# Value products of two attentions emitted per pair of heads, alternating between the two 64-row halves of the output

## The chip, the core and the metric

The kernel runs on one NeuronCore of one Trainium2 chip. The metric is the device time of one execution in microseconds. Before the change it is 2310.92 us, the median of 3 runs (2307.32 to 2318.86). Engines are called PE (TensorE; PEld is its weight load), DVE (VectorE), ACT (ScalarE), POOL (GpSimd) and SP (SyncE, which issues most transfers).

## What is computed

Two transformer blocks run one after the other over 256 tokens of width 1024, with 256 context tokens. The first block has two layers (an even one with an mLSTM mixer, an odd one with windowed attention), each between two gated feed-forward networks. The second block joins a latent attention with a state-space scan and ends in a convolutional feed-forward network. The change touches the two attentions:

- Odd layer: 16 query heads of 64 dimensions share 4 key and value heads. Each block of 128 queries sees 256 context keys and up to 256 keys of its own stream (a window of 128 each way). The softmax has one more term per head, a learned sink.
- Latent attention: 16 heads with scores over 64 + 32 dimensions, values of 64 dimensions, 512 keys, and no sink.

In both, one head's output for 128 queries is

```
p = softmax(scores)        # 128 queries x 512 keys
out = p @ v                # 512 keys x 64 value dimensions
```

and the outputs of all heads go through an output projection.

## The kernel before, in words

Nearly all matrix products of the program are made of three products of float32r halves (`mac3`, lines 580 to 584: high by high, high by low, low by high). The transposes and the value products work on plain float32.

**A unit of attention** is one head with 128 queries. Each attention has 32 units, made by the local function `unit` (line 1558 in `odd`, line 2195 in `mla`) in the order pair of heads, query block `qb`, head `s` of the pair, so that the units `s = 0` and `s = 1` of a pair follow each other. `attention` (line 1416) runs them as a software pipeline whose stages are written in a string:

```
AO = "s0 e1 n1 t3 v4 f0"
```

In iteration i it emits `st0` of unit i (the scores, lines 1567 to 1570 or 582 to 584, then the row maximum on DVE, L1427), `st1` of unit i-1 (the exponential on ACT, L1436, and with a sink L1439 and L1440), `st2` of unit i-1 (reciprocal and scaling on DVE, L1444 and L1445), `st3` of unit i-3 (four transposes on PE, L1451, and their copy out of PSUM on ACT, L1453, which makes the tile `PT`), `st4` of unit i-4 (the value products) and then other work that was put beside the attention (`fill`: in `odd` the modulation of the second block's context, in `mla` the projections of queries, keys and values and their weights).

**Value products** (L1578 and L2213): four matmuls of a unit, one for each block of 128 keys. The stationary operand is a slice of 64 columns of `V`, the moving operand a slice of 128 columns of `PT`, both 128 partitions of float32. The result has 64 rows, in the lower half (rows 0 to 63) of the PSUM tile `po` for `s = 0` and in the upper half (rows 64 to 127) for `s = 1`:

```
for b in range(4):
    nc.tensor.matmul(po[64 * s:64 * s + 64, ...], lhsT=V[b][:, kv * 64:kv * 64 + 64],
                     rhs=PT[:, b * P:(b + 1) * P], start=b == 0, stop=b == 3, tile_position=(0, 64 * s), ...)
```

The profile shows each such float32 matmul as two instructions, so a unit's value products are eight. After 8 units `po` is full and is split into float32r halves for the output projection (`split`, lines 604 and 605).

A third place writes into halves of PSUM in the same way: `y` in `ssd` (lines 2335 to 2350) computes outputs of the state-space scan from the same kinds and sizes of operands (L2349). Its innermost loop is the one over `s`, so its matmuls go to the lower and the upper half in turn.

**Order and buffers.** The engines' instructions are placed when the program is built: instructions are taken in the order of emission as far as a model of that moment holds them ready, so an instruction whose input is late is passed by later ones. Blocks of [128, 512] (`b2`, 42 buffers, line 334) hold `PT`, the probabilities, keys, queries and values; `mm` (5 banks) and `aux` (2 banks) are the PSUM tiles of scores and transposes. `po` takes one bank of `bg` and one of `mm` in turn (line 395).

Of the kernel before, what the change touches and what calls it, by code (L numbers as in the profile page):

```python
# [56 lines left out]
P = 128  # L57
# [11 lines left out]
# ---------------------------------------------------------------- host layout  # L69
# [44 lines left out]
def _pack_tok(w):  # L114
    """Pieces of 4 blocks of rows by 512 columns, the column halves one after the other."""
    kb = w.shape[0] // P
    parts = []
    for c in range(2):
        for k0 in range(0, kb, 4):
            t = w.reshape(kb, P, D)[k0:k0 + 4, :, c * 512:(c + 1) * 512].transpose(1, 0, 2)  # L120
            parts.append(np.ascontiguousarray(t).reshape(-1))
    return np.concatenate(parts)
# [174 lines left out]
# ---------------------------------------------------------------- the program  # L297
# [5 lines left out]
class Beat:  # L303
    """Emission order of work that waits on long chains: after(k, f) emits f once k more blocks of products are out."""
# [23 lines left out]
class Prog:  # L328
# [18 lines left out]
    @contextmanager  # L347
    def in_order(self):
        """Each compute engine issues what this block emits in the order of its emission."""
        ins = self.nc.cur_bb.bb.instructions  # L350
        n = len(ins)
        yield
        self.tails = {}
        for i in list(ins[n:]):
            if i.engine != mybir.EngineType.SP:
                if i.engine in self.tails:
                    self.issue_behind(i, self.tails[i.engine])
                self.tails[i.engine] = i

    @contextmanager  # L360
    def behind_now(self):
        """What this block emits is issued behind what has been emitted."""
        ins = self.nc.cur_bb.bb.instructions
        n = len(ins)
        last = {i.engine: i for i in ins[-200:]}
        yield
        for i in list(ins[n:]):
            if i.engine in last:
                self.issue_behind(i, last[i.engine])

    @contextmanager
    def behind(self):
        """What this block emits is issued behind the last block in order."""
        ins = self.nc.cur_bb.bb.instructions
        n = len(ins)
        yield
        for i in list(ins[n:]):
            if i.engine in self.tails:
                self.issue_behind(i, self.tails[i.engine])

    # ---- tiles
# [13 lines left out]
    def po(self):  # L395
        """Accumulators of attention outputs, alternating between two pools."""
        self.npo = getattr(self, "npo", 0) + 1
        if self.npo % 2:
            return self.gp.tile([P, 512], F32, tag="bg", name=self.name("bg"))
        return self.mm()  # L400

    def scope(self, name):
        """A pool for one phase; self.sp is the pool that phase allocates from."""
        self.sp_es = ExitStack()
        self.sp = self.sp_es.enter_context(self.tc.tile_pool(name=name, bufs=1))
# [43 lines left out]
    # ---- modulation vectors  # L449
# [5 lines left out]
    def mods(self, ci, w, bias, M, i0, cnt, post):  # L455
        """Steps that compute modulation vectors i0 .. i0+cnt-1 of M, one weight slab each."""
# [41 lines left out]
    def mods_acc(self, ci, w, bias, M, i0, cnt, post, nctx):  # L498
        """Like mods, with the products summed over weight slabs on VectorE and only the last sum, over
        partitions, on the tensor engine. nctx: how many of the vectors the context stream uses."""  # L500
# [42 lines left out]
    def tick(self, n=1.0):  # L543
        """Emit background steps worth n."""
# [11 lines left out]
    # ---- weights: hi + lo, each exact in float32r  # L556
    def wload(self, src, nk, width, pool=()):
        """pool: the pieces whose lo part GpSimd computes."""
# [27 lines left out]
    def pair3(self, ps, W, X, first, last):  # L586
        """Both halves of one block of rows, the products that need the lo part of X behind the others."""
# [19 lines left out]
    # ---- rms statistics of one half (256 tokens), features on partitions  # L607
# [23 lines left out]
    def rstd2(self):  # L631
        """r1 = rms(h)^-1 and r12 = r1 * rms(h * fin * r1)^-1, as columns r12, r12, r1, r1.

        With a = mean h^2 + eps and b = mean (h fin)^2: r12 = (b + eps a)^-1/2."""
# [15 lines left out]
    def chunk(self, half, t, c):  # L650
        """Features 512 c.. of the tokens 128 t.., tokens on partitions, in the place of 2 blocks of h."""
        return self.h[:, 4 * c + 2 * t:4 * c + 2 * t + 2, HS[half]]

    def finish_first(self):
        """h_x = rms(h_x) * fin, the result of the first block, with tokens on partitions from here on."""
# [12 lines left out]
    def gain(self, i, cs=range(2)):  # L668
        """Gate times gain of the second block, along the free axis."""
# [24 lines left out]
    def tok_gemm(self, acts, src, evac, tail=None):  # L694
        """Products with tokens on partitions: evac(t, c, ps) of tokens 128 t.. and columns 512 c.. .

        tail(products) takes over before the last pieces, where products(t) emits those of t."""
# [39 lines left out]
    def modulate(self, acc, srcs, sc, sh, X, n=D):  # L737
        """X[k] = split(src[k] * sc[k] * rstd + sh[k]) over one half."""
# [46 lines left out]
    def start(self, X):  # L785
        """Loads, the first norm and its modulation (a quarter of the features at a time), and the products of
        the first two hidden blocks over each quarter as it becomes ready. Returns their accumulators."""
# [135 lines left out]
    # ---- swiglu over both streams  # L923
# [74 lines left out]
    # ---- one-stream feed forward: act(j, psum[:, 2, 256]) -> (hi, lo)  # L998
# [40 lines left out]
    # ---- even mixer  # L1039
    def even(self, X, M, half_done):  # L1040
# [18 lines left out]
        # q, k (convolved, feature-major); gates first  # L1059
# [12 lines left out]
        k = []  # L1072
# [25 lines left out]
        # output gate and spatial gating unit, in pieces that run between the mlstm steps  # L1098
# [84 lines left out]
        def out_s(m):  # L1183
            """The part of the output that the gating unit feeds."""
# [11 lines left out]
        def out_m(half, m):  # L1196
            """The part of the output that the mlstm feeds, over one half."""
# [26 lines left out]
    def mlstm_gates(self, G):  # L1224
        """Row-wise gate arithmetic. Rows 0-3 forward heads, rows 32-35 backward heads."""
# [60 lines left out]
    def mlstm(self, q, k, v, gates, hs):  # L1286
# [22 lines left out]
        def prep(n):  # L1309
            """What a step needs apart from the running state."""  # L1310
# [73 lines left out]
    # ---- odd mixer (x stream queries; keys of both streams)  # L1384
# [6 lines left out]
    def rope_mul(self, x, rows, tab, n):  # L1391
        """x [rows, n, 256] f32 in SBUF -> its two rotated terms."""
# [23 lines left out]
    def attention(self, units, pre, order):  # L1416
        """Software-pipelined attention. A unit is 128 queries of one head against 512 keys:
        (scores() -> PSUM, (sink, -sink) columns or None, values(PT)); pre[n] runs before unit n's scores."""
# [54 lines left out]
    def odd(self, X, M, before, half_done):  # L1473
# [84 lines left out]
        def unit(a_, g, qb, s):  # L1558
# [14 lines left out]
            def values(PT):  # L1573
                if (g % 2, qb, s) == (0, 0, 0):
                    hold["po"] = self.po()
                po = hold["po"]
                for b in range(4):
                    nc.tensor.matmul(po[64 * s:64 * s + 64, (g % 2) * 256 + qb * P:(g % 2) * 256 + qb * P + P],  # L1578
                                     lhsT=V[b][:, kv * 64:kv * 64 + 64], rhs=PT[:, b * P:(b + 1) * P],
                                     start=b == 0, stop=b == 3, tile_position=(0, 64 * s), skip_group_check=True)  # L1580
                if (g % 2, qb, s) == (1, 1, 1):
# [25 lines left out]
    # ---- second block: conv5 + silu of one xbc feature block  # L1607
# [13 lines left out]
    def ssd_gates(self, ps):  # L1621
        """Rows 0-15 forward dt, rows 32-47 backward dt, [128, 256 tokens]."""
# [13 lines left out]
        # per-token columns: -acum, dt, dt * exp(acum_end - acum); per-chunk exp(acum_end) on all partitions  # L1636
# [33 lines left out]
    def xs_tok(self, xs, c, g):  # L1670
        """Token-major heads of group g, chunk c, in PSUM [128 tokens, 8, 64]."""
# [31 lines left out]
    def in_half(self, srcname, i, b, X, W):  # L1703
        """One 128-feature block of an input projection; W keeps the weights of the slab."""
# [28 lines left out]
    def block2_setup(self):  # L1733
        nc = self.nc
        # silu(t) = u (1 + tanh u) with u = t / 2: the convolution yields u
# [22 lines left out]
    def norm_later(self, bt, k, acc, srcs, sc, X, n):  # L1758
        """X = split(src * sc * rstd), its statistics k beats from now, the rest a beat after that."""
# [18 lines left out]
    def ctx_stats(self):  # L1778
        """Steps that leave 1 / rms of the second block's context in rc."""
# [11 lines left out]
    def ctx_path(self):  # L1791
        """Everything of the second block's context that its x stream reads, in pieces."""
# [329 lines left out]
    def mla(self, CQ, tab):  # L2122
# [72 lines left out]
        def unit(pair, qb, s):  # L2195
# [10 lines left out]
            def values(PT):  # L2206
                if (pair % 2, qb, s) == (0, 0, 0):
                    hold["po"] = self.po()
                po = hold["po"]
                hd = (2 * pair + s) % 8  # L2210
                col = (pair % 2) * 256 + qb * P
                for tb in range(4):
                    nc.tensor.matmul(po[64 * s:64 * s + 64, col:col + P], lhsT=V[pair // 4, tb][:, hd * 64:hd * 64 + 64],  # L2213
                                     rhs=PT[:, tb * P:(tb + 1) * P], start=tb == 0, stop=tb == 3,
                                     tile_position=(0, 64 * s), skip_group_check=True)
                if (pair % 2, qb, s) == (1, 1, 1):
# [54 lines left out]
    def ssd(self, xs, B, Cm, ac, TA, DD, DE):  # L2271
        """State-space scan of the x stream, in pieces: cb, xd_a(g, c), xd_b(g, c), unit(n), mix(n), y(n)."""
# [62 lines left out]
        def y(n):  # L2335
            """Outputs of the units n and n + 1."""
# [22 lines left out]
    # ---- the whole computation  # L2359
    def run(self):  # L2360
# [104 lines left out]
        # the final norm of the first block folds into the norm of the second  # L2465
# [36 lines left out]
```

## Time and profile before

| | |
|---|---|
| runs shown | 2307.32, 2310.92, 2318.86 us; median 2310.92 |
| profiled execution, span from first to last instruction | 2305.9 us; its own device time is not listed beside it |
| median over the span | 5.0 us |
| mean granted TensorE clock | 0.991 of 2.4 GHz |
| PE, DVE, ACT busy | 97%, 68%, 42% of the span |
| odd attention, first to last value product | 1459.3 to 1532.0 us |
| latent attention, first to last value product | 1988.6 to 2079.7 us |

The span and the stretches are of one profiled execution. A share of busy time is an average over stages with different limits, so the two attentions are read by themselves, in stretches and in the order of PE's instructions. In a timeline a row with xN stands for N instructions in a row on one line; the duration of such a row reaches to the end of the last one, and since matmuls overlap in the pipeline, the time that a row takes from the stream is the distance from its start to the next row's start.

### The profile page before, as it was taken

Reading aid. Unit: us, or ns where it says so; the run is one execution under the profiler, and the core shown is the slowest. Engines: PE = TensorE matmul, PEld = TensorE weight load, DVE = VectorE, ACT = ScalarE, POOL = GpSimd, SP = SyncE. Lnnn points to the kernel's source line nnn. Section 1 sums busy time; section 2 is a strip of 40 time slices with the busy share of each in tenths; the row PEclk is TensorE's granted clock in tenths of the full one; section 3 lists DMA queues with packets and bytes.
Section 4 is the critical chain, followed back from the end, with each engine's and each line's share of the span. In section 5 each row is a group of like instructions: output and inputs, shape, how many; then the busy total and the mean of one; then the engine's idle time right before and its main releaser. Section 6 shows DMA issues by size and latency. Waiting matters only on the chain.

```text
span 2305.9 us, 33864 instructions
## 1 busy us (share of the span) xinstructions
PE 2247.0 (97%) x13706; PEld 1956.2 (85%) x13706; DVE 1564.9 (68%) x2447; ACT 975.2 (42%) x1651; POOL 166.7 (7%) x185
## 2 busy tenths in 40 slices
PE   7999999999899999999999999999999899999998
PEld 6888888888898888898878889789999788888997
DVE  5887774734897666468748647757556898666664
ACT  4222223544542222243222335656445566665553
POOL 0000000001300000000000002101000553000000
PEclk8999999999999999999999999999999999999999
DMA  7665552221145455325657623114554323213553
GB/s 266 218 232 182 185 204 83 92 101 74 56 160 187 155 192 183 146 92 201 242 173 285 231 92 115 57 56 169 184 183 160 133 88 122 85 60 126 184 175 120
DMA packets 58076, 348.54 MB, mean 151 GB/s; under 512 B 6464, under 2 KB 10048, under 8 KB 22848
## 3 DMA queue, kind: packets, MB, share of 16 engines
q1 hardware_dynamic: 56544, 344.22, 42.1%
q8 instruction: 108, 1.77, 0.3%
q0 software_dynamic: 512, 1.05, 0.2%
q10 hardware_dynamic: 864, 1.11, 0.2%
q14 instruction: 48, 0.39, 0.0%
HBM read 343.73 MB, written 1.05 MB: 150 GB/s over the span
## 4 chain that ended last, share of the span: by engine, by line
PE 76%; issue 13%; DVE 5%; POOL 3%; ACT 1%; DMA 1%; SPq 0%; POOLq 0%; DVEq 0%; ACTq 0%
PE mm L582 21%; PE mm L584 20%; PE mm L583 20%; PE mm L591 6%; PE ax L1451 1%; DVE wl L575 1%; POOL b L1727 1%; PE bg L531 1%; PE bg L1578 1%; PE bg L2213 1%; PE mm L1578 1%; PE mm L2213 1%; DMA b<-mod 1%; POOL b L1728 1%; DVE acc L616 0%
## 5 line engine op out<-in xcount | busy, mean ns | idle before, releaser
L582 PE MATMUL mm<-b,wh 128*128 128x512 f32 (+1 forms) x2764 | 958.5, 348 | 3.6 <-DVE c L1617 1.9
L584 PE MATMUL mm<-b,wl 128*128 128x512 f32 (+1 forms) x2764 | 947.7, 344 | 3.6 <-DVE wl L575 3.5
L583 PE MATMUL mm<-b,wh 128*128 128x512 f32 (+1 forms) x2764 | 949.5, 344 | 0.0
L575 DVE TENSOR_TENSOR wl<-wr,wh 128x1024 fp32r<-128x1024 f32 (+2 forms) x474 | 553.7, 1173 | 392.0 <-ACT wh L574 385.5
L574 ACT CAST wh<-wr 128x1024 fp32r<-128x1024 f32 (+2 forms) x474 | 473.7, 1006 | 575.8 <-PE mm L583 389.8
L582 PEld LDWEIGHTS mm<-b,wh 128*128 128x128 f32 x2764 | 527.0, 191 | 78.3 <-issue 8.5
L584 PEld LDWEIGHTS mm<-b,wl 128*128 128x128 f32 x2764 | 526.1, 191 | 65.7 <-DVE wl L575 5.0
L583 PEld LDWEIGHTS mm<-b,wh 128*128 128x128 f32 x2764 | 527.3, 191 | 61.0 <-issue 1.9
L522 DVE SCALAR_TENSOR_TENSOR ma<-mr,cs,ma 128x1024 f32<-128x1024 f32 x252 | 311.5, 1278 | 32.9 <-DMA mr<-ada 28.8
L591 PE MATMUL mm<-b,wh 128*128 128x256 f32 x1408 | 254.5, 283 | 0.0
L591 PEld LDWEIGHTS mm<-b,wh 128*128 128x128 f32 x1408 | 220.3, 192 | 0.2 <-ACT b L604 0.2
L591 PE MATMUL mm<-b,wl 128*128 128x256 f32 x704 | 184.4, 283 | 0.0
L591 PEld LDWEIGHTS mm<-b,wl 128*128 128x128 f32 x704 | 135.5, 192 | 0.0
L927 ACT ACTIVATE s<-mm 128x512 f32<-128x512 f32 x66 | 39.5, 599 | 222.2 <-PE mm L584 222.1
L582 PE MATMUL mm<-wh,b 128*128 128x512 f32 (+1 forms) x264 | 100.1, 380 | 1.9 <-ACT b L604 1.9
L583 PE MATMUL mm<-wl,b 128*128 128x512 f32 (+1 forms) x264 | 99.5, 377 | 0.0
L584 PE MATMUL mm<-wh,b 128*128 128x512 f32 (+1 forms) x264 | 99.3, 377 | 0.0
L629 POOL TENSOR_TENSOR rr<-rv,nhalf 128x2 f32<-128x2 f32 x15 | 15.6, 1043 | 991.6 <-DVE rv L628 991.6
L604 ACT CAST b<-s 128x512 fp32r<-128x512 f32 x70 | 43.2, 617 | 73.4 <-DVE s L928 64.9
L928 DVE TENSOR_TENSOR s<-s,mm 128x512 f32<-128x512 f32 x66 | 45.2, 684 | 40.3 <-PE mm L584 40.3
L1427 DVE TENSOR_REDUCE mx<-mm 128x1 f32<-128x512 f32 x64 | 43.8, 687 | 31.9 <-PE mm L1570 17.5
L983 DVE SCALAR_TENSOR_TENSOR h<-mm,M,h 128x256 f32<-128x256 f32 x144 | 59.6, 476 | 7.5 <-PE mm L584 7.5
(357 smaller groups left out, 2072.8 us busy)
## 6 DMA issues: line engine op xcount, KB each, us to landing
wr<-win SPq DMA_DIRECT2D x88, 1024.0 KB, 4.8
mr<-ada SPq DMA_DIRECT2D x56, 1024.0 KB, 4.9
wr<-wout SPq DMA_DIRECT2D x40, 768.0 KB, 4.4
mr<-mod SPq DMA_DIRECT2D x26, 1024.0 KB, 5.0
wr<-b_up SPq DMA_DIRECT2D x22, 1024.0 KB, 4.9
wr<-wout SPq DMA_DIRECT2D x14, 1024.0 KB, 4.8
wr<-b_xbc SPq DMA_DIRECT2D x11, 1024.0 KB, 4.9
wr<-b_down SPq DMA_DIRECT2D x10, 1024.0 KB, 4.9
```

Of the source, the lines that this page charges most:

```text
L522: nc.vector.scalar_tensor_tensor(hold["a"][s][:, c], raw[:, c], v, hold["a"][s][:, c], op0=ALU.mult, op1=ALU.add)
L574: nc.scalar.copy(hi, r)
L575: (nc.gpsimd if k0 // kk in pool else nc.vector).tensor_sub(lo, r, hi.bitcast(F32))
L582: nc.tensor.matmul(ps, lhsT=ah, rhs=bh, start=first, stop=False)
L583: nc.tensor.matmul(ps, lhsT=ah, rhs=bl, start=False, stop=False)
L584: nc.tensor.matmul(ps, lhsT=al, rhs=bh, start=False, stop=last)
L591: nc.tensor.matmul(ps[:, HS[q]], lhsT=l[:, P * q:P * q + P], rhs=r, start=first and q == 0 and l is wh and r is xh, stop=last and q == 1 a ...
L928: nc.vector.tensor_mul(s, s, pu)
L983: nc.vector.scalar_tensor_tensor(h[:, m, c], ps[:, c], M[:, ig, m, half:half + 1], h[:, m, c], op0=ALU.mult, op1=ALU.add)
L1427: nc.vector.tensor_reduce(mx, S[u], axis=AX.X, op=ALU.max, negate=True)
L1578: nc.tensor.matmul(po[64 * s:64 * s + 64, (g % 2) * 256 + qb * P:(g % 2) * 256 + qb * P + P], lhsT=V[b][:, kv * 64:kv * 64 + 64], rhs=PT[: ...
L2213: nc.tensor.matmul(po[64 * s:64 * s + 64, col:col + P], lhsT=V[pair // 4, tb][:, hd * 64:hd * 64 + 64], rhs=PT[:, tb * P:(tb + 1) * P], st ...
```

## The change

`values` of a unit `s = 0` now issues nothing and only keeps its `PT`. `values` of the unit `s = 1` issues the products of both: for each block of 128 keys first the one into the lower half, then the one into the upper half. The number of matmuls, their operands and sizes are the same. `po` is taken and split at the same places in the order of units. Other lines of the diff drop comments and docstrings; they change no instruction.

```diff
@@ odd, unit
             def values(PT):
-                if (g % 2, qb, s) == (0, 0, 0):
+                if s == 0:
+                    hold["PT"] = PT
+                    return
+                if (g % 2, qb) == (0, 0):
                     hold["po"] = self.po()
                 po = hold["po"]
+                col = (g % 2) * 256 + qb * P
                 for b in range(4):
-                    nc.tensor.matmul(po[64 * s:64 * s + 64, (g % 2) * 256 + qb * P:(g % 2) * 256 + qb * P + P],
-                                     lhsT=V[b][:, kv * 64:kv * 64 + 64], rhs=PT[:, b * P:(b + 1) * P],
-                                     start=b == 0, stop=b == 3, tile_position=(0, 64 * s), skip_group_check=True)
-                if (g % 2, qb, s) == (1, 1, 1):
+                    for z, t in enumerate((hold["PT"], PT)):
+                        v = (2 * a_ + z) * 64
+                        nc.tensor.matmul(po[64 * z:64 * z + 64, col:col + P], lhsT=V[b][:, v:v + 64],
+                                         rhs=t[:, b * P:(b + 1) * P], start=b == 0, stop=b == 3,
+                                         tile_position=(0, 64 * z), skip_group_check=True)
+                if (g % 2, qb) == (1, 1):
...
@@ mla, unit
             def values(PT):
-                if (pair % 2, qb, s) == (0, 0, 0):
+                if s == 0:
+                    hold["PT"] = PT
+                    return
+                if (pair % 2, qb) == (0, 0):
                     hold["po"] = self.po()
                 po = hold["po"]
-                hd = (2 * pair + s) % 8
                 col = (pair % 2) * 256 + qb * P
                 for tb in range(4):
-                    nc.tensor.matmul(po[64 * s:64 * s + 64, col:col + P], lhsT=V[pair // 4, tb][:, hd * 64:hd * 64 + 64],
-                                     rhs=PT[:, tb * P:(tb + 1) * P], start=tb == 0, stop=tb == 3,
-                                     tile_position=(0, 64 * s), skip_group_check=True)
-                if (pair % 2, qb, s) == (1, 1, 1):
+                    for z, t in enumerate((hold["PT"], PT)):
+                        hd = (2 * pair + z) % 8
+                        nc.tensor.matmul(po[64 * z:64 * z + 64, col:col + P],
+                                         lhsT=V[pair // 4, tb][:, hd * 64:hd * 64 + 64], rhs=t[:, tb * P:(tb + 1) * P],
+                                         start=tb == 0, stop=tb == 3, tile_position=(0, 64 * z), skip_group_check=True)
+                if (pair % 2, qb) == (1, 1):
```

## Rows read from the trace of the kernel before

**Rows 1.** The page: span, busy time and instructions by engine, clock in 40 slices.

```profile
span 2305.9 us, 33864 instructions
...
PE 2247.0 (97%) x13706; PEld 1956.2 (85%) x13706; DVE 1564.9 (68%) x2447; ACT 975.2 (42%) x1651; POOL 166.7 (7%) x185
...
PEclk8999999999999999999999999999999999999999
```

**Rows 2.** The page, the chain that ended last: its shares by engine.

```profile
PE 76%; issue 13%; DVE 5%; POOL 3%; ACT 1%; DMA 1%; SPq 0%; POOLq 0%; DVEq 0%; ACTq 0%
```

**Rows 3.** Stretches: us, busy PE, PEld, DVE, ACT, POOL, clock, DMA share, GB/s.

```profile
1459.27:1531.96 72.68, 72.68 (x486) 54.84 (x486) 46.93 (x164) 48.56 (x129) 0.00 (x0) 1.00 0.04 16
1988.59:2079.66 91.07, 91.07 (x583) 73.63 (x583) 60.03 (x127) 60.71 (x130) 6.39 (x12) 1.00 0.21 67
```

**Rows 4.** PE's timeline in the odd attention: start us, duration us, instruction, count.

```profile
1506.21 0.50 PE L1567 MATMUL mm<-b,b 128*128 128x512 f32 x1
1506.56 0.23 PE L1568 MATMUL mm<-cstb 128*128 128x128 bf16 x1
...
1507.14 0.60 PE L1451 MATMUL ax<-cst,b 128*128 128x128 f32 x4
1507.67 1.09 PE L1578 MATMUL bg<-b,b 128*64 128x128 f32 x8
1508.69 0.50 PE L1567 MATMUL mm<-b,b 128*128 128x512 f32 x1
```

**Rows 5.** PE's timeline, the same in the latent attention.

```profile
2060.59 0.60 PE L1451 MATMUL ax<-cst,b 128*128 128x128 f32 x4
2061.12 1.09 PE L2213 MATMUL bg<-b,b 128*64 128x128 f32 x8
...
2062.94 0.60 PE L1451 MATMUL ax<-cst,b 128*128 128x128 f32 x4
```

**Rows 6.** Waits in the odd attention: who waited for whom, us in total, times, longest.

```profile
DVE mx L1427 <- PE mm L1570: 17.5, 21, 2.6
ACT b L1453 <- PE ax L1451: 17.0, 22, 1.3
...
PEld bg L1578 <- ACT b L1453: 0.7, 2, 0.4
```

**Rows 7.** PE's timeline in the odd attention, where a unit's products came apart.

```profile
1493.33 0.65 PE L1578 MATMUL mm<-b,b 128*64 128x128 f32 x4
1493.92 0.66 PE L1451 MATMUL ax<-cst,b 128*128 128x128 f32 x4
```

**Rows 8.** PE's timeline in the state-space scan, the alternating products of L2349.

```profile
1882.85 1.97 PE L2349 MATMUL mm<-b,b 128*64 128x128 f32 x32
1884.74 0.49 PE L728 MATMUL ax<-cst,rr 128*128 128x128 f32 x2
```

**Rows 9.** PE's timeline at the odd attention's end, two units in one run.

```profile
1530.31 1.71 PE L1578 MATMUL mm<-b,b 128*64 128x128 f32 x16
1531.96 0.38 PE L583 MATMUL mm<-b,wh 128*128 128x256 f32 x1
```

**Rows 10.** PE's timeline in the odd attention, transposes with scores right behind them.

```profile
1480.08 0.60 PE L1451 MATMUL ax<-cst,b 128*128 128x128 f32 x4
1480.44 0.47 PE L1567 MATMUL mm<-b,b 128*128 128x512 f32 x1
1480.76 0.23 PE L1568 MATMUL mm<-cstb 128*128 128x128 bf16 x1
```

**Rows 11.** Busy us by stretch, columns as in rows 3: quiet, dense, scan.

```profile
1506.21:1523.52 17.31, 17.31 (x113) 12.95 (x113) 10.78 (x37) 10.82 (x30) 0.00 (x0) 1.00 0.01 1
...
1468.59:1490.30 21.72, 21.72 (x144) 16.38 (x143) 17.98 (x60) 17.36 (x46) 0.00 (x0) 1.00 0.11 39
1990.00:2060.00 70.00, 70.00 (x437) 56.80 (x436) 48.67 (x101) 48.67 (x105) 5.46 (x10) 1.00 0.26 84
...
1880.00:1950.00 70.00, 70.00 (x678) 65.45 (x677) 61.45 (x102) 44.75 (x108) 26.28 (x22) 1.00 0.32 109
```

## The prediction

> **What bounds the kernel.** I read the page first: PE is busy 97% of a span of 2305.9 us, DVE 68%, ACT 42%, and the clock stands at its upper level (2.4 GHz) nearly throughout [rows 1]. The chain that ended last is PE for 76% and issue for 13% [rows 2]. Whole-program shares say nothing of one stage, so I took busy time by stretch, from the first to the last value product of each attention: PE has no idle time in either (72.68 of 72.68 us, 91.07 of 91.07), while ACT and DVE are busy 65 to 67% of each, at clock 1.00 [rows 3]. PE's timeline shows why. In the odd attention a unit is scores, mask, four transposes and eight value products back to back, 2.48 us from one L1567 to the next (1506.21 to 1508.69) [rows 4]; in the latent one 2.35 us between transposes (2060.59 to 2062.94) [rows 5]. The waits point the same way: in the odd attention DVE waits 17.5 us for scores and ACT 17.0 us for transposes, PE only 0.7 us, twice, for a copied PT [rows 6]. So time taken out of PE's stream comes out of the end, until ACT or DVE takes over.
>
> **The products themselves.** No instruction is added or removed: 64 units of eight value matmuls, 128*64 by 128x128 (512), before and after. What counts is what they take from PE's stream. One unit's eight take 1.02 us, start to next start (1507.67 to 1508.69; the latent form, x8 of the same shape, lasts the same 1.09 us) [rows 4, 5]. Eight last 1.09 us and four 0.65 us [rows 4, 7], so each further one into the same half costs 0.11 us. The alternating order stands in this kernel already: L2349, of the same shape, with 32 matmuls into the two halves in turn, lasts 1.97 us and takes 1.89 us (1882.85 to 1884.74) [rows 8]. One behind another, 32 would last 0.65 + 28 x 0.11 = 3.73 us; 0.65 + 12 x 0.11 = 1.97 us is what sixteen would. So two matmuls run in the time of one. Sixteen alternating ones should then last as eight do, 1.09 us, and take 1.02 us where the two units now take 2.04 us: **1.02 us less per pair**. The lower bound of this gain is the run of sixteen at the odd attention's end, where two units follow each other without alternation: 1.65 us (1530.31 to 1531.96) [rows 9], which would leave 0.39 us. I take the L2349 value, as it has the same shape, halves and loop order.
>
> **The switches between kinds of matmul.** PE's bursts of value products become half as many. From the transposes' start to the second score matmul a stream with a burst takes 0.53 us (1507.14 to 1507.67), the burst, and 0.35 us (as 1506.21 to 1506.56) [rows 4]; without a burst 0.36 and 0.32 us (1480.08, 1480.44, 1480.76) [rows 10]. A burst thus costs 0.20 us beside its products, and every pair saves one.
>
> **Sum on PE.** 32 pairs x (1.02 + 0.20) = 39.0 us. The last pair of each attention already stands as one run, at least in the odd one [rows 9], and saves 1.65 - 1.02 = 0.6 instead of 1.2: minus 1.2 us for both. That leaves 38 us.
>
> **What takes over.** The odd stretch would shrink from 72.7 to about 54 us, with 48.6 us of ACT and 46.9 us of DVE work in it (90% and 87%); the latent one from 91.1 to 72, with 60.7 and 60.0 us (84%) [rows 3]. In the state-space scan DVE is busy 61.45 of 70 us (88%) and PE still has no idle time [rows 11], so 88% is bearable. The dense part of the odd attention is not under it: 21.7 us minus its 9 bursts (4.5 pairs, 5.5 us) is 16.2 us, with 17.98 us of DVE work [rows 11]. Its least loss is 1.8 us; at 88% it lasts 20.4 us, a loss of 4.2, and ACT over the whole odd stretch at 88% needs 55.2 us, 1 to 2 us more than PE. The latent one's dense part comes to 70 - 11 x 1.22 = 56.6 us with 48.67 us on each (86%) [rows 11]: nothing. Bounds 2 and 6 us, and I take the upper end, 6, since scores now come in two distances (about 1.3 and 2.5 us) and the softmax chain has less slack. What hides that chain: from the scores of a unit to its transposes three units pass, 7.4 us now and about 5.6 us after; in the quiet part ACT and DVE need 10.8 us for 7 units, 1.55 us each, against 1.87 us of PE [rows 11]. If that cover goes, PE waits at the transposes.
>
> **The order.** The instructions' order is set when the program is built, by readiness, and in the trace a unit's eight were sometimes cut in two by other work (x4, transposes, then the rest) [rows 7]. The products of s = 1 need a PT that was copied less than one iteration before: between that unit's transposes and the pair's products stand one unit's scores (0.93 us, 1506.21 to 1507.14) and transposes, 1.3 us together [rows 4]; before, the other unit's products, 1.0 us, stood there too. Where the model finds it late, the four products of s = 0 are placed ahead and the pair does not alternate. That costs 1.65 - 1.02 = 0.63 us a pair [rows 9]: nothing at best, 20 us if all 32 go so. I take 5 pairs, 3 us, near the lower end, because the copy now waits only for its transposes [rows 6].
>
> Moved with the products: no DMA and no wait on SP or POOL, whose queues see none of this; the split of po comes behind the same unit as before. The b2 block of an s = 0 unit is held one unit longer; I cost that at nothing, since no ACT instruction in the waits waits for a value product to free a block [rows 6]; without that cover see rival C.
>
> **Forecast.** -38 + 6 + 3 = -29 us. Against the profiled span, 2305.9 - 29 = 2276.9 us; the median of the runs is 5.0 us above that span, so **2282 us**. A measurement of this kernel can tell about 0.5% (11.6 us) from no change.
>
> **Rivals.**
>
> A. *Softmax or order eats most of it.* The pairs come out unalternated throughout (+20 us instead of 3) with the same 6 us of ACT and DVE: -38 + 20 + 6 = -12 us, 2299 us; half of that is about 2290. For it: the cut unit [rows 7] and 90% on ACT. Against it: nearly all bursts before are whole, and the state-space scan holds 88%. Between 2290 and 2300: chance 0.20, a tenth of it within 0.5%. The Trainium skill warns in "TensorEngine Tiling (Array Packing)", section PSUM Bottleneck, that packing small matmuls speeds up PE but not the copies out of PSUM, which may become the bottleneck; here these are the exponential and the PT copy on ACT, and the trace agrees that ACT comes near.
>
> B. *The two halves do not run beside each other here.* Then sixteen cost 1.02 + 8 x 0.11 = 1.90 us, a pair saves 2.04 - 1.90 + 0.20 = 0.34 us, together 11 us: 2300 us, within 0.5%. Against it stands L2349 [rows 8]. Chance 0.03. The Trainium skill's rule in "TensorE: Matmul & The Clock Gate", Part 3, "What overlaps and what doesn't", speaks for it: a weight load overlaps running matmuls only when the row group differs, and both halves here use all 128 rows. The trace does not agree: L2349's products, each with a weight load of its own, come at 0.06 us each.
>
> C. *Slower.* With one more PT held, the 42 blocks run out, and the exponential of a later unit (L1436) waits for the pair's products. PE then idles for exponential, scaling, transposes and copy in a row. It decides from 1.2 us of idle a pair, where the gain is used up; at 2 us a pair it is 32 x 2 - 38 = +26 us, 2337 us. No wait of that kind stands among the waits [rows 6]. Chance 0.04.
>
> D. *No change worth measuring for another reason*, above all that the new placement costs elsewhere what it gains here; 2305 us. PE's chain is 76% of the span, so a loss must hit PE's stream. Chance 0.03.
>
> The forecast's own case (2270 to 2290) has 0.70. Faster: 0.70 and 0.18 of A, 0.88. Same: the rest of A, B and D, 0.02 + 0.03 + 0.03 = 0.08. Slower: C, 0.04. The range reaches from all of 38 us with 2 us lost (2275 us) and some 5 us for runs below, 2270, to rival A's end, 2299.
>
> **What would show it.** Right: L1578 and L2213 in 32 runs of 16 that take about 1.02 us; stretches of about 58 and 74 us; ACT's waits for L1451 and DVE's for L1570 much shorter; PE waits of some us for L1445 or L1453. Wrong: runs of 16 at 1.65 us or in pieces (A), at 1.90 (B), L1436 waiting for L1578 (C), or both stretches shorter by 19 us and the span not (D).

## The result, and the profile after

The changed kernel takes **2285.02 us** (median of four runs, 2280.91 to 2288.52) where the kernel before, on the same chip, takes 2311.39 us (four runs, 2307.32 to 2318.86). The ratio is 0.9878, 95% interval 0.9857 to 0.9899: 26.4 us less by the medians. The profiled execution shown below has 2284.95 us of its own, with a span of 2283.2. The forecast was 2282 us, faster.

In the changed kernel the value products are L1584 (odd attention), L2223 (latent attention) and, unchanged, L2359 (scan; L2349 before). The page of the changed kernel, its first lines and the shares of the chain that ended last:

```profile
span 2283.2 us, 33862 instructions
PE 2224.3 (97%) x13706; PEld 1935.4 (85%) x13706; DVE 1563.4 (68%) x2447; ACT 973.1 (43%) x1651; POOL 167.6 (7%) x185
...
PE 76%; issue 13%; DVE 5%; POOL 3%; ACT 2%; DMA 1%; SPq 0%; POOLq 0%; DVEq 0%; ACTq 0%
```

Beside [rows 1, 2] nothing seems to have happened: the same number of PE instructions, the same 97%, the same chain. A whole-program page can't show this change; PE was full before and is full after, with less in it. The two stretches show it. Changed kernel, from the first to the last value product of the odd and of the latent attention, columns as in [rows 3]:

```profile
1462.19:1523.26 61.07, 61.07 (x491) 43.99 (x490) 46.75 (x164) 47.51 (x129) 0.00 (x0) 1.00 0.05 19
1980.48:2057.95 77.47, 77.47 (x583) 61.77 (x582) 57.73 (x125) 59.08 (x129) 5.48 (x10) 1.00 0.23 77
```

72.68 us became 61.07, and 91.07 became 77.47 (58 and 74 were forecast). The work of ACT and DVE is what it was (47.51 and 46.75 us in the odd stretch, now 78% and 77% of it), and PE still has no idle time in either stretch. The waits of the odd stretch, changed kernel (who waited for whom, us in total, times, longest):

```profile
ACT b L1453 <- PE ax L1451: 9.9, 17, 1.5
DVE mx L1427 <- PE mm L1570: 5.6, 11, 1.2
...
PEld bg L1584 <- ACT b L1453: 1.0, 3, 0.4
...
PEld mm L1584 <- ACT b L1453: 0.4, 1, 0.4
```

Against [rows 6] the engines behind PE have lost their slack in part, ACT's waits for transposes from 17.0 to 9.9 us and DVE's for scores from 17.5 to 5.6, but PE has not begun to wait for them: 1.4 us in all for a copied PT, as good as nothing.

PE's timeline of the changed kernel, a pair of the odd attention whose products stand in one run (columns as in [rows 4]):

```profile
1504.31 0.60 PE L1451 MATMUL ax<-cst,b 128*128 128x128 f32 x4
1504.84 1.09 PE L1584 MATMUL bg<-b,b 128*64 128x128 f32 x16
1505.86 0.50 PE L1567 MATMUL mm<-b,b 128*128 128x512 f32 x1
...
1508.05 0.60 PE L1451 MATMUL ax<-cst,b 128*128 128x128 f32 x4
1508.58 1.09 PE L1584 MATMUL bg<-b,b 128*64 128x128 f32 x16
1509.60 0.50 PE L1567 MATMUL mm<-b,b 128*128 128x512 f32 x1
```

Sixteen instructions (eight float32 matmuls) take 1.02 us (1504.84 to 1505.86), exactly as eight did [rows 4]. A pair's period is 3.74 us (1505.86 to 1509.60) where two units took 2 x 2.48 = 4.96.

But not every pair comes out so. The same timeline some 20 us earlier, and in the latent attention:

```profile
1484.87 0.60 PE L1451 MATMUL ax<-cst,b 128*128 128x128 f32 x4
1485.40 1.09 PE L1584 MATMUL mm<-b,b 128*64 128x128 f32 x14
1486.42 0.23 PE L1568 MATMUL mm<-cstb 128*128 128x128 bf16 x1
...
1487.77 0.43 PE L1584 MATMUL mm<-b,b 128*64 128x128 f32 x2
1488.13 0.23 PE L1568 MATMUL mm<-cstb 128*128 128x128 bf16 x1
...
2045.06 0.60 PE L1451 MATMUL ax<-cst,b 128*128 128x128 f32 x4
2045.59 0.43 PE L2223 MATMUL mm<-b,b 128*64 128x128 f32 x2
2045.95 0.50 PE L582 MATMUL mm<-b,b 96*128 96x512 f32 x1
```

Here one matmul (two instructions) stands by itself and takes 0.36 us (1487.77 to 1488.13; 2045.59 to 2045.95), and the remaining fourteen take 1.02 us (1485.40 to 1486.42), as long as sixteen. That is plain from the halves: seven matmuls are left, four of them in the same half, and those four set the length. So the one sent ahead saves nothing where it is missing, and its 0.36 us is all extra. Counted over PE's timeline, from a run's start to the start of what follows:

| | runs of value products | their time |
|---|---|---|
| before, odd + latent | 34 + 31 = 65 | 32.6 + 32.1 = 64.7 us |
| changed, odd + latent | 31 + 25 = 56 | 21.3 + 19.6 = 40.9 us |
| if every pair were one run of 16 | 32 | 32 x 1.02 = 32.6 us |

In the changed kernel 20 of the 32 pairs are cut like that, 10 are whole and two are in three pieces; in all, 23 matmuls stand alone. Cutting costs 40.9 - 32.6 = 8.3 us, which is 23 x 0.36.

**Where the 26 us lie.** Odd attention: from the first L1567 to the first value product of the scan it is 434.2 us before (1448.6 to 1882.8) and 422.1 after (1451.5 to 1873.6), 12.1 less. From there to the end of the span, 423.1 before and 409.6 after, 13.5 less. Together 25.6 us. The spans differ by 22.7 only, since in the profiled execution shown after, the odd attention happened to begin 2.9 us later, from work ahead of it that both kernels share. A section of one profiled execution is good to some 3 us only: in the runs with one attention alone (below), where the other attention is as before, that other section takes 437.0 us (odd) and 424.7 us (latent) against 434.2 and 423.1.

### The profile page after: what moved, and what is told of

It is laid out like the page before. It is cut to its first block, busy times and chain, and to the rows that moved or that the text cites. A ratio compares the mean times of both kernels' runs of the same rounds, so it can differ in the third digit from the quotient of the medians.

```text
span 2283.2 us, 33862 instructions
## 1 busy us (share of the span) xinstructions
PE 2224.3 (97%) x13706; PEld 1935.4 (85%) x13706; DVE 1563.4 (68%) x2447; ACT 973.1 (43%) x1651; POOL 167.6 (7%) x185
## 3 DMA queue, kind: packets, MB, share of 16 engines
q10 hardware_dynamic: 864, 1.11, 0.2%
## 4 chain that ended last, share of the span: by engine, by line
PE 76%; issue 13%; DVE 5%; POOL 3%; ACT 2%; DMA 1%; SPq 0%; POOLq 0%; DVEq 0%; ACTq 0%
PE mm L582 21%; PE mm L584 21%; PE mm L583 21%; PE mm L591 6%; PE ax L1451 1%; DVE wl L575 1%; PE bg L531 1%; POOL b L1733 1%; POOL b L1734 1%; DMA wr<-wout 1%; DVE acc L616 0%; POOL rr L629 0%; PE bg L1584 0%; PE mm L1584 0%; DMA mr<-mod 0%
## 5 line engine op out<-in xcount | busy, mean ns | idle before, releaser
L629 POOL TENSOR_TENSOR rr<-rv,nhalf 128x2 f32<-128x2 f32 x15 | 15.7, 1044 | 982.6 <-DVE rv L628 982.6
L763 ACT ACTIVATE b<-v,M 128x256 fp32r<-128x256 f32 x88 | 40.4, 501 | 47.9 <-DVE v L759 47.8
```

Source lines behind the costliest of these rows:

```text
L763: nc.scalar.activation(xh, v, AF.Identity, bias=sh)
```

## The experiments

**Why are pairs cut?** The program is placed in the order of emission as far as the model of that moment holds instructions ready. The changed loop emits the product of `s = 0` first, whose PT is a unit older. That one is ready early and is passed ahead; the next one needs the young PT of `s = 1`. If so, it is enough to emit the product of the young PT first (both attentions):

```
-                    for z, t in enumerate((hold["PT"], PT)):
+                    for z, t in ((1, PT), (0, hold["PT"])):
```

> Both attentions as in the change, but in each block of keys the product of s = 1 (whose PT is the younger one) is emitted ahead of that of s = 0. Theory (order): the change lost some 12 us of its 38 because the first product of s = 0 was ready early and was placed alone, a run of 2 and a run of 14 instead of one of 16; now the runs are whole, some 34 runs instead of 56, 22 x (0.36 + 0.2) = 12 us less than the change, about 2273 us, stretches of about 55 and 71 us. Rival (ACT and DVE): they set the pace already, PE gets idle time instead, and the time stays within 4 us of the change's 2285. Rival (new wait): a whole run now waits for the copy of the younger PT, some 0.3 us x 32 = 10 us of PE idle at L1453, no gain.

Measured: 2277.64 us (2272.92 to 2279.50), ratio 0.9846 (0.9831 to 0.9860) against before at 2312.24. PE's timeline of this kernel, the place that was cut before, and one in the latent attention:

```profile
1482.96 0.63 PE L1451 MATMUL ax<-cst,b 128*128 128x128 f32 x4
1483.52 1.09 PE L1584 MATMUL mm<-b,b 128*64 128x128 f32 x16
1484.54 0.23 PE L1568 MATMUL mm<-cstb 128*128 128x128 bf16 x1
...
2030.18 1.09 PE L2223 MATMUL bg<-b,b 128*64 128x128 f32 x16
2031.20 0.50 PE L582 MATMUL mm<-b,wh 128*128 128x512 f32 x1
```

All 16 latent pairs and 14 of the 16 odd ones are now one run; the 34 runs take 16.9 + 16.4 = 33.3 us, 7.6 less than in the change. The median fell by 7.4 us from the changed kernel's. So the cut was a matter of which product is emitted first, and nothing of the data has to arrive sooner for it. The 12 us expected did not come in full: 4.4 of them were put on 22 fewer switches between kinds of matmul, and the scores, masks and transposes beside the products, counted from start to start in the same way, take 2.4 us less (ledger below). Of the 10.0 us counted so the medians show 7.4.

**Is it the alternation, or only that two units' products stand together?** The same, with the halves one after the other: the four products of `s = 1`, then the four of `s = 0`:

```
-                for b in range(4):
-                    for z, t in ((1, PT), (0, hold["PT"])):
+                for z, t in ((1, PT), (0, hold["PT"])):
+                    for b in range(4):
```

> As x1_late_first, but the four products of s = 1 are emitted ahead of the four of s = 0, so a pair stands in one run without alternating. Theory (two halves run side by side only when they alternate): a run of 16 takes about 1.65 us instead of 1.02, 32 x 0.62 = 20 us more than x1_late_first, about 2293 us. Rival (grouping alone gives the gain, by fewer switches): the same time as x1_late_first. Rival (no overlap at all without alternation): runs of 1.90 us, 28 us more, about 2301 us.

Measured: 2294.32 us (2292.57 to 2296.18), ratio 0.9921 (0.9906 to 0.9936). PE's timeline of this kernel:

```profile
1502.70 0.60 PE L1451 MATMUL ax<-cst,b 128*128 128x128 f32 x4
1503.22 1.58 PE L1584 MATMUL bg<-b,b 128*64 128x128 f32 x16
1504.74 0.51 PE L1567 MATMUL mm<-b,b 128*128 128x512 f32 x1
```

The run takes 1.51 us (1503.22 to 1504.74), between alternating (1.02) and what one half costs (next). The kernel loses 16.7 us against the first experiment, and 32 x (1.51 - 1.02) = 15.7. So the order of the sixteen alone is worth that, about half of the gain. The half that stays comes from the end of one group running beside the start of the other, as the starts within the run show. The same row, read only up to 1503.715 us and up to 1504.11 us:

```profile
1503.22 0.76 PE L1584 MATMUL bg<-b,b 128*64 128x128 f32 x5
1503.22 1.15 PE L1584 MATMUL bg<-b,b 128*64 128x128 f32 x12
```

Five instructions start within the first 0.49 us, as slowly as in one half (0.11 us from one to the next). Then seven start within 0.4 us, and the last four come 0.11 us apart again. So the second group begins at 1503.72, while the last three instructions of the first are still to come, and from there to the end it takes the 1.02 us of any eight: 0.49 + 1.02 = 1.51.

**Do the halves matter?** A pair is here two query blocks of one head, so that the sixteen alternate between two column ranges of the same 64 rows:

```
-                    for z, t in ((1, PT), (0, hold["PT"])):
-                        nc.tensor.matmul(po[64 * z:64 * z + 64, col:col + P], ..., tile_position=(0, 64 * z), ...)
+                    for z, t in ((1, PT), (0, hold["PT", s])):
+                        col = (g % 2) * 256 + z * P
+                        nc.tensor.matmul(po[64 * s:64 * s + 64, col:col + P], ..., tile_position=(0, 64 * s), ...)
```

> As x1_late_first, but the pair that alternates is made of the two query blocks of one head, so both products of a turn go to the same 64 rows of the output (different columns); the result is the same. Theory (it is the two halves that run side by side): a run of 16 takes 1.02 + 8 x 0.11 = 1.90 us, 28 us more than x1_late_first, about 2301 us, still some 6 to 11 us under the kernel before by the fewer switches. Rival (any alternation of two accumulations helps): the same time as x1_late_first.

Measured: 2306.09 us (2299.52 to 2309.31), ratio 0.9967 (0.9954 to 0.9980). PE's timeline of this kernel:

```profile
1502.14 1.96 PE L1584 MATMUL bg<-b,b 128*64 128x128 f32 x16
1504.03 0.66 PE L1451 MATMUL ax<-cst,b 128*128 128x128 f32 x4
```

1.89 us a run (1502.14 to 1504.03), as rival B reckoned it (1.90), and 28.5 us over the first experiment, where 32 x (1.89 - 1.02) = 27.8. Two accumulations stand open at once in the same rows of one bank here, so this kernel leaves out a part of the sums, which its expectation had not foreseen: by the Trainium skill ("PSUM — Partial Sum Buffer", The four PSUM rules) the start of the second makes the first one overwrite what it had. No trace here shows the overwriting. Number, shape and order of the instructions are not touched by that, and the time can be read as it stands. It is 6.2 us under the kernel before, with 30 runs of value products in place of 65.

**Each attention alone.** The products of the other one stay as before.

> The change in the odd attention alone; the latent one as in the kernel before. Theory (each attention keeps what PE's stream saves in it): the odd stretch shrinks by some 12 us, as in the changed kernel, and the latent one not at all: about 2299 us. Rival (the gain of one attention is made up by what follows): the span moves by less than 6 us, or by all 26.

> The change in the latent attention alone; the odd one as in the kernel before. Theory: the latent stretch shrinks by some 13 us, the odd one not at all: about 2298 us; with x5_odd_alone the two gains add up to the 26 us of the whole change. Rival (they are not independent): the sum of both differs from 26 us by more than 8.

Measured, both beside before at 2312.04: odd alone 2298.09 us (2294.65 to 2302.71), ratio 0.9942 (0.9924 to 0.9960); latent alone 2299.14 us (2297.65 to 2301.12), ratio 0.9945 (0.9930 to 0.9960). The two stretches, first with odd alone, then with latent alone:

```profile
1459.18:1520.25 61.07, 61.07 (x490) 43.99 (x489) 46.76 (x164) 47.52 (x129) 0.00 (x0) 1.00 0.06 19
1978.90:2069.97 91.07, 91.07 (x583) 73.62 (x583) 60.04 (x127) 60.69 (x130) 6.38 (x12) 1.00 0.21 67
```

```profile
1459.33:1532.02 72.69, 72.69 (x487) 54.84 (x486) 46.94 (x164) 48.56 (x129) 0.00 (x0) 1.00 0.05 16
1994.30:2071.78 77.48, 77.48 (x584) 61.78 (x583) 57.72 (x125) 59.09 (x129) 5.46 (x10) 1.00 0.23 77
```

Each edit shortens its own stretch to the very length it has in the full change and leaves the other as it was. 13.95 + 12.90 = 26.9 us, the 26.4 of the change within what is measured: the parts add, and neither gives back what the other gains.

**How much room have ACT and DVE?** The prediction gave 6 us to them. In the changed kernel the copy of PT (L1453) is made twice, 64 further copies of 0.59 us on ACT, 38 us in all:

```
             nc.scalar.copy(PT, pt)
+            nc.scalar.copy(PT, pt)
```

> The changed kernel, with each copy of the transposes into PT (L1453) made twice on ACT: 64 x 0.59 = 38 us of ACT work more in the two stretches, where ACT has 13.6 and 18.4 us idle. Theory (PE set the pace in the changed kernel, ACT had room): most of it is hidden, and the time rises only by what ACT lacks, 38 - 32 = 6 us, and some 3 us for runs cut more often (27 instead of 22), to about 2294 us, at most 2305 with waits in the chain. Rival (ACT already set the pace): all of it shows, 2285 + 38 = 2323 us.

Measured: 2293.78 us (2289.82 to 2295.91), ratio 0.9919 (0.9904 to 0.9934), 8.8 us over the changed kernel. The two stretches:

```profile
1461.45:1529.59 68.14, 65.16 (x515) 47.17 (x514) 48.41 (x158) 61.25 (x159) 0.00 (x0) 1.00 0.06 19
1982.62:2066.93 84.31, 83.89 (x601) 64.80 (x600) 59.08 (x125) 73.20 (x160) 5.47 (x10) 1.00 0.22 71
```

With ACT at 90% (61.25 of 68.14) and 87% (73.20 of 84.31) PE idles 3.0 and 0.4 us; 27 matmuls stand alone here against 23, another 4 x 0.36 = 1.4 us; the rest of the 8.8 us was not located. So 38 us more on ACT were three quarters covered, and the changed kernel itself, at 78%, was not near the point where ACT takes over.

**Longer runs.** Four units' products in one run of 32, the youngest pair first (the loop `for y in (1, 0)` over the query blocks outside the two loops of the first experiment):

> As x1_late_first, but four units (both heads and both query blocks) in one run of 32, youngest first, so half as many runs again and up to four PT tiles held. Theory (order and switches): 15 fewer runs x 0.2 us = 3 us less than x1_late_first, about 2270 us. Rival (ACT and DVE): between two runs PE now needs only about 5.1 us for four units where ACT and DVE need 6.2, so PE waits about 1 us per four units, 16 x 1 = 16 us at most, and the time is above x1_late_first by up to 10 us.

Measured: 2276.62 us (2271.97 to 2280.04), ratio 0.9843 (0.9828 to 0.9859). Stretches (the third row is a part of the odd one), waits in the odd one, and PE's timeline there:

```profile
1465.28:1518.45 53.17, 50.27 (x462) 39.13 (x461) 41.13 (x143) 41.49 (x114) 0.00 (x0) 0.97 0.06 21
1982.42:2051.25 68.83, 68.01 (x561) 57.02 (x561) 54.55 (x116) 53.89 (x119) 5.46 (x10) 1.00 0.26 85
1480.50:1483.80 3.30, 3.30 (x28) 2.64 (x26) 2.50 (x10) 2.62 (x9) 0.00 (x0) 0.50 0.51 156
```

```profile
PEld ax L1451 <- ACT b L1436: 1.9, 1, 1.9
PEld mm L1585 <- ACT b L1453: 1.8, 3, 1.2
```

```profile
1478.62 0.63 PE L1451 MATMUL ax<-cst,b 128*128 128x128 f32 x4 [1.45 <-DVE b L1445]
1480.25 1.00 PE L1585 MATMUL mm<-b,b 128*64 128x128 f32 x8 [1.01 <-ACT b L1453]
1481.18 1.11 PE L1451 MATMUL ax<-cst,b 128*128 128x128 f32 x4
...
1489.91 1.97 PE L1585 MATMUL mm<-b,b 128*64 128x128 f32 x32
1491.82 0.23 PE L1568 MATMUL mm<-cstb 128*128 128x128 bf16 x1
```

Thirty-two take 1.91 us against 2 x 1.02, so little more is gained per product, and in the odd attention PE now waits, 2.9 us in the stretch (53.17 less 50.27), once 1.45 us at the transposes for L1445: the place that the prediction named for when the cover of the softmax chain goes. Behind this wait and the next one (1.01 us for L1453) the granted clock falls to 0.50, the lower of its two levels (1.2 GHz), from 1480.5 to 1483.8 us, and four transposes last 1.11 us there, against 0.63 in the row before it fell. So the waits cost more than their own length. Whether the kernel is faster than the first experiment can't be told (the intervals lie on each other).

**Both together:** odd attention as in the first experiment, latent as in the last.

> The odd attention as in x1_late_first (pairs), the latent one as in x4_four_units (four units in a run). Theory (four units are worth it where PE has other work to put between, as the projections in the latent attention, and PE waits for ACT where it has none, as in the odd one): some 1 to 3 us under both, about 2275 us. Rival (run length no longer matters): 2277 us, not to be told from x1_late_first.

Measured: 2275.12 us (2271.99 to 2281.77), ratio 0.9844 (0.9826 to 0.9863). The lowest median, but not to be told from the two it is made of. The first experiment, one swapped loop, is the version to keep: 2277.64 us, faster than the kernel before and, with its four runs (2272.92 to 2279.50) all under the changed kernel's four (2280.91 to 2288.52), than the changed one, though these two did not run side by side.

## Why the prediction was right

The ledger of the prediction and of the traces, in us. The trace's own total is the 25.6 us of the two sections; the first experiment by the same two sections gives 16.6 (1452.5 to 1870.1 is 417.6) and 15.6 (1870.1 to 2277.6 is 407.5), 32.2 in all.

| step | predicted | changed kernel | young product first |
|---|---|---|---|
| products | -32 | -23.8, of which order +8 | -31.4, of which order under +1 |
| switches | -6 | -2.0 | -4.4 |
| ACT and DVE take over | +6 | 0 | +0.2 |
| order | +3 | (in the first two rows) | |
| not located | | +0.2 | +3.4 |
| sum | -29 | -25.6 | -32.2 |

The products' row is the time of runs counted on PE's timeline (64.7 to 40.9, and to 33.3). The switches' row is counted in the same way, without idle time, over the instructions of the two attentions that stand between the runs, the scores, masks and transposes of the 64 units: 47.18 + 40.63 = 87.81 us before, 46.46 + 39.40 = 85.86 in the changed kernel, 45.00 + 38.45 = 83.45 in the first experiment. This count repeats: where one attention is left as before, it is 47.17 (odd) and 40.63 (latent). ACT and DVE's row is PE's idle time in the stretches, and the last row is what is then left of the sections' total, which is no better than their 3 us.

- **What bounds the kernel** was right: PE without idle time, so what leaves its stream leaves the end. The runs with one attention alone show it, each stretch by itself.
- **The products, 1.02 us a pair**, were right to the hundredth: sixteen take 1.02 us. Taking the price from L2349, with the same shape, halves and order, was the right choice over the 1.65 us of the run at the odd attention's end; 1.65 would have halved the gain, and that run takes longer than even a grouped one (1.51) because its second half waited for its PT (last section).
- **The switches, 0.20 us a burst**, were somewhat too dear, and the number of bursts was wrong. Thirty-one runs fewer (65 to 34) bring 4.4 us in the first experiment, 0.14 us each, nearly all of it in the transposes, where the prediction had found it (0.53 against 0.36 us, [rows 4, 10]). In the changed kernel only nine runs fell away, as the order left 56 where 32 were forecast, and they bring 2.0 us. By the medians the first experiment gains 34.6 us, interval 32 to 39 (0.9831 and 0.9860 of 2312); the counted rows give 35.6.
- **ACT and DVE, 6 us**, did not come. The term was the upper end of its bounds (2 to 6), worked out for a stretch of 54 us. The stretch came to 61, with ACT at 78%; and where the first experiment did bring the odd stretch to 54.21 us, PE was busy 54.19 of them with ACT at 45.55 (84%) and DVE at 44.66. The prediction's "88% is bearable" was too careful as a limit: in the dense part of that stretch, 24 us long, DVE is busy 95% and ACT 94%, and PE still 23.98 us. What the bound is was seen only with longer runs or doubled copies. The rows of the first experiment, odd, latent, and the dense part of the odd one:

```profile
1465.04:1519.25 54.21, 54.19 (x486) 41.13 (x485) 44.66 (x154) 45.55 (x124) 0.00 (x0) 1.00 0.06 21
1980.18:2052.69 72.51, 72.31 (x575) 59.15 (x574) 56.38 (x122) 56.62 (x126) 6.79 (x10) 1.00 0.25 81
1464.00:1488.00 24.00, 23.98 (x208) 17.45 (x208) 22.74 (x82) 22.53 (x62) 0.00 (x0) 1.00 0.08 21
```

- **The order, 3 us**, was the right mechanism in the wrong size and form. The prediction had the four products of `s = 0` placed ahead, at 0.63 us, for 5 pairs. In truth a single product, mostly the very first, went ahead in 22 pairs, 23 products at 0.36 us: 8 us, and some 2 us more in switches (85.86 against 83.45). The reason given for few pairs, that a copy waits only for its transposes [rows 6], speaks of the chip, whereas the placement is made by the model when the program is built. The unit that was already cut in the trace of before [rows 7] was the better sign.

So terms of 9 us against the change were forecast (6 and 3). What was paid instead is 8 us in the products and 2 in the switches for the order, and about 2 more because a switch was priced too dear. That the forecast is only 3 us off is luck in part, since these errors have opposite signs; the bound on PE and the price of the products are not luck.

**The rivals.** A came in part: order took some 10 us, not 20, and softmax nothing. The bottleneck that the Trainium skill warns of ("TensorEngine Tiling (Array Packing)", PSUM Bottleneck) did not arrive at this size: PE has no idle time in the changed kernel's stretches, and 3.0 us in the odd one only when the copies are doubled and ACT is busy 90%. B is ruled out: with the same halves the run takes B's 1.89 us, with two halves 1.02. C, a wait of L1436 for L1584, appears in no list of waits. D fell with the runs of each attention alone.

## What to carry to other kernels

Matmuls that fill only 64 of the output's rows should alternate between the halves instruction by instruction: grouping them by half gave up half of the gain here (2294 against 2278 us), and writing to one half four fifths of it (2306). Where products of an older and a younger operand are interleaved and a scheduler places them by readiness, emit the one with the younger operand first; otherwise the old one is sent ahead alone and the run is cut. Look for it in the lengths of the runs on the timeline: x14 and x2 where x16 was meant.

## What was not expected of the hardware

- Sixteen products grouped by half take 1.51 us in the second experiment, but 1.65 us in the run of the kernel before [rows 9] and 1.54 us at the end of its latent attention (2078.12 to 2079.66). From the second group's first start to the end it is 1.02 us in all three; that start comes 0.49, 0.63 and 0.52 us after the run's. In the two runs of the kernel before it follows the copy of the unit's PT by 0.05 us (1530.94, 2078.64), so there the group waited for its operand. The two copies, on ACT:

```profile
1530.30 0.59 ACT L1453 COPY b<-ax 128x512 f32<-128x512 f32 x1 [1.18 <-PE ax L1451]
2078.00 0.59 ACT L1453 COPY b<-ax 128x512 f32<-128x512 f32 x1 [0.96 <-PE ax L1451]
```

- Both halves use all 128 rows of the operands, and yet two products run in the time of one, 1.02 against 1.89 us for sixteen; in the changed kernel the second starts 0.01 us behind the first (1504.85 and 1504.84). The Trainium skill's rule in "TensorE: Matmul & The Clock Gate" (Part 3, What overlaps and what doesn't), that a weight load overlaps only matmuls of another row group, is not borne out by these runs: the output half decided whether two products ran side by side.
- A matmul of 64 columns that stands alone among the wider ones takes 0.36 us of PE's stream, nearly three times the 0.13 us (1.02 / 8) that one takes in an alternating run.
